# Two gate tiles of a hybrid decoder layer stored without their sigmoid, which is applied when they are loaded

## The chip, the core and the metric

The kernel runs on one core of a Trainium2 chip. Its engines are TensorE (PE, matrix products; PEld is its weight load), VectorE (DVE), ScalarE (ACT, elementwise functions by tables), GpSimd (POOL) and SyncE (SP, which here issues most transfers). Each engine takes its own instructions in order and waits on semaphores for the others. The metric is the device time of one execution in microseconds; lower is better.

## The reference

One decoder layer over 1024 positions of width 1024, in float32: a half feed-forward, two token mixers side by side, another half feed-forward, and a gated input embedding. The change lies in the gates that join the two mixers:

```python
fq, fk, fv, f_logit, sq, sk, sv, g_fox, g_sb = split_columns(h @ w_in[i])
...
y_fox = forgetting_attention(fq, fk, fv, log_f)      # 8 heads, softmax with forget gates
y_sb = stick_breaking_attention(sq, sk, sv)          # 8 heads, sigmoids and a running product
merged = (jax.nn.sigmoid(g_fox) * (y_fox @ w_branch_fox[i])
          + jax.nn.sigmoid(g_sb) * (y_sb @ w_branch_sb[i]))
x = x + merged @ w_out[i]
```

`g_fox` and `g_sb` have 1024 columns each. The forgetting heads (called fox heads in the kernel) need exponentials for their softmax; the stick-breaking heads need sigmoids; both gates need sigmoids.

## The kernel before

Everything is float32 split into a high and a low part, so that a product is three products of parts; the split is a cast on ScalarE and a subtraction on VectorE or GpSimd. The stages are: first feed-forward, mixer inputs, attention, merging of the branches, output projection, second feed-forward, embedding.

*Gates.* The 2048 gate columns are 16 tiles of 128 columns by 1024 positions, numbered 0 to 7 for `g_fox` and 8 to 15 for `g_sb`. Tiles 0 to 11 are made ahead of attention. Tiles 12 to 15 are made inside attention, as filler: `g_units(m)` makes tile `m` in two halves of 512 positions. For each half, 24 products (L807) gather in a PSUM bank, ScalarE turns the bank into a tile PT by a sigmoid (L926), and SP stores PT to the DRAM buffer `gates` (L927). The next user of that PSUM bank waits for L926.

*Attention.* Sixteen heads follow each other, heads 0 to 7 forgetting, 8 to 15 stick-breaking. In a fox head, scores (L1050, L1051) are added and their extremes taken on VectorE (L1055), ScalarE takes the exponential of a row block (L1061), VectorE the reciprocal of its sum (L1062), GpSimd multiplies (L1063). The weights are transposed on TensorE (L1109) into one of two PSUM banks of tag `pt`, ScalarE casts the bank to the high part (L1111), VectorE subtracts to get the low part (L1117) and so frees the bank, and TensorE multiplies with the values (L1135). Sums of two parts of an output are joined by L1161 and L1164. The stacks of queries and keys of later heads are filled by transposes (L897), L884, L885 and small copies on SP's queue (L887).

To keep TensorE fed between the dependent steps of a head, each head has a list `fill` of other units of work, of which some products are issued at each step. Tile 12 stands in the list of head 3, tile 13 in those of heads 6 and 7, tiles 14 and 15 in those of stick-breaking heads.

*Order.* The feed-forwards and the first gates are in an order written out by hand. In attention and the merging stage a planner orders the instructions of each engine by priorities and its own costs; for TensorE the program's order is pinned (`pe`), and for ScalarE and VectorE parts of the stick-breaking heads, the gate function among them (`order("act", ...)`). Tiles come from pools with tags and a fixed number of buffers (PT has 4, T 6, KL and Q 2); a tile waits for the last reader of the buffer that it gets.

*Tables.* ScalarE computes a function from a loaded table. Where the next function is not in the table in place, the build puts a load (ACT_TABLE_LOAD) ahead of it. A copy or cast needs none.

*Merging.* After attention, `load_gate(m)` loads tile 8+m into a buffer of tag T, or KL for m = 4 and Q for m = 5 (L1495). For each m the products of the stick-breaking branch (L1397) gather in a bank, VectorE multiplies the loaded gate with it (L1515) and adds the forgetting branch (L1516). The forgetting branch itself has its gates loaded by L1402 and multiplied by L1403.

Of the kernel before, what the change touches and what calls it, by code (L numbers as in the profile page):

```python
# [13 lines left out]
AF = mybir.ActivationFunctionType  # L14
# [8 lines left out]
KD = D // P  # L23
# [13 lines left out]
def tile_hybrid_decoder_layer(  # L37
# [6 lines left out]
    nc = tc.nc  # L44
# [11 lines left out]
    def slot(tag, shape, dt=F32):  # L56
        pad = -shape[-1] % 16
        t = sb.tile([*shape[:-1], shape[-1] + pad], dt, tag=tag, bufs=BUFS[tag], name=nm(tag))
        return t[:, :, :shape[-1]] if pad else t

    def stat(shape, tag, bufs=4):
        return st.tile(shape, F32, tag=tag, bufs=bufs, name=nm(tag))
# [3 lines left out]
    def bank(tag):  # L66
        return pp.tile([P, 512], F32, tag=tag, bufs=PSUM[tag], name=nm("ps"))

    def ps1():
        ring[0] += 1  # L70
        return bank(("pt", "pf", "pt", "pf")[ring[0] % 4])
# [11 lines left out]
    def order(key, ins):  # L83
        prev = last.get(key)
        if prev is not None and not manual[0]:
            tc.add_manual_dep(ins.ins, prev.ins.name, NOSYNC, reason="order")
        last[key] = ins
# [23 lines left out]
    def wload(pieces, nk, n, tags=("WH", "WL"), eng_lo=nc.gpsimd):  # L111
        return wsplit(wraw_load(pieces, nk, n), nk, n, tags, eng_lo)
# [31 lines left out]
    def kp(w):  # L144
        return w.rearrange("(k p) n -> p k n", p=P)
# [645 lines left out]
    def mix_nat(cols, tags):  # L791
        n = sum(b - a for a, b in cols)
        return [wload([kp(win)[:, 4 * kh:4 * kh + 4, a:b] for a, b in cols], 4, n, tags[kh]) for kh in range(2)]

    def nat_steps(ps, t, w, n, hT):
        i = 0
        for a, b in ((0, 0), (1, 0), (0, 1)):
            for k in range(KD):
                pe(nc.tensor.matmul(ps[:, :n], hT[t // 4](a, k)[:, (t % 4) * P:(t % 4 + 1) * P], w[k // 4][b][:, k % 4, :n], start=(i == 0), stop=(i == 23)))  # L799
                i += 1  # L800
                yield 0.109

    def feat_steps(ps, half, w):
        i = 0
        for a, b in ((0, 0), (0, 1), (1, 0)):
            for k in range(KD):
                pe(nc.tensor.matmul(ps[:], w[a][:, k, :], hT[half](b, k), start=(i == 0), stop=(i == 23)))  # L807
                i += 1
                yield 0.216
# [3 lines left out]
    def add_load(cell, fn):  # L813
        cell["i"] = len(loads)
        loads.append([cell, fn])

    def weights(cell, ahead=2):
        for i in range(cell["i"] + ahead):
            if i < len(loads) and loads[i][1] is not None:
                loads[i][0]["w"] = loads[i][1]()  # L820
                loads[i][1] = None
        return cell["w"]
# [9 lines left out]
    def v_units(col, extra, cell, new_bank=fill_bank):  # L832
        n = 256 + extra
        add_load(cell, lambda: mix_nat([(col, col + n)], NAT))

        def unit(t):
            weights(cell)
            if t == 0:
                cell["v"] = slot("X", [P, NT, 4, P], F32R)
            ps = new_bank()  # L840
            yield from nat_steps(ps, t, cell["w"], n, hT)
            v2 = cell["v"]
            src = ps[:, :256].rearrange("p (h d) -> p h d", h=4)
            split(v2[:, t, :, 0:HD], v2[:, t, :, HD:P], src, nc.scalar, nc.vector)
            if extra:
                nc.vector.tensor_copy(lfs[:, t, :], ps[:, 256:264])
        return [(24 * 0.109, unit(t)) for t in range(NT)]

    def fox_qk_units(pair, cell, tags=NAT, sq_tag="PT", new_bank=fill_bank):
        add_load(cell, lambda: mix_nat([(FQ + pair * P, FQ + pair * P + P), (FK + pair * P, FK + pair * P + P)], tags))  # L850

        def unit(t):
            weights(cell)
            if t == 0:
                cell["n"] = [slot("RN", [P, 4, 2, 2, HD]) for _ in range(2)]
                cell["ss"] = [stat([P, 4, 4], "qkss", 4) for _ in range(2)]
            half, q = divmod(t, 4)
            ps = new_bank()
            yield from nat_steps(ps, t, cell["w"], 256, hT)
            N = cell["n"][half]  # L860
            src = ps[:, :256].rearrange("p (s h d) -> p s h d", s=2, h=2)
            sq = slot(sq_tag, [P, 256])
            nc.scalar.activation(sq[:].rearrange("p (h s d) -> p s h d", s=2, h=2), src, AF.Square)
            nc.scalar.copy(N[:, q].rearrange("p h s d -> p s h d"), src)  # L864
            nc.vector.reduce_sum(cell["ss"][half][:, q, :], sq[:].rearrange("p (g d) -> p g d", g=4), axis=AX.X)
            if q == 3:
                ss = cell["ss"][half][:].rearrange("p a b -> p (a b)")
                nc.vector.tensor_scalar(ss, ss, 1.0 / HD, EPS, ALU.mult, ALU.add)
                nc.gpsimd.tensor_tensor(ss, ss, mhalf[:], ALU.pow)
                nv = N[:].rearrange("p a h s d -> p (a h s) d")  # L870
                nc.gpsimd.tensor_mul(nv, nv, ss.unsqueeze(2).broadcast_to([P, 16, HD]))
        return [(24 * 0.109, unit(t)) for t in range(NT)]
# [30 lines left out]
    def sb_stack_units(head, out_cell):  # L903
        c0 = head * HD

        add_load(out_cell, lambda: wload([kp(win)[:, :, SQ + c0:SQ + c0 + HD], kp(win)[:, :, SK + c0:SK + c0 + HD]], KD, P))

        def unit(half):
            weights(out_cell)
            if half == 0:  # L910
                out_cell["st"] = new_stacks()
            ps = bank("pf")
            yield from feat_steps(ps, half, out_cell["w"])
            fill_stacks(out_cell["st"], ps, slice(half * 512, half * 512 + 512))
        return [(24 * 0.216, unit(0)), (24 * 0.216, unit(1))]

    def g_units(m, new_bank=fill_bank):
        cell = {}

        add_load(cell, lambda: wload([kp(win)[:, :, GFOX + m * P:GFOX + m * P + P]], KD, P))  # L920

        def unit(half):
            ps = new_bank()
            yield from feat_steps(ps, half, weights(cell))
            g = slot("PT", [P, 512])
            order("act", nc.scalar.activation(g[:], ps[:], AF.Sigmoid))  # L926
            nc.sync.dma_start(gd[m, :, half * 512:half * 512 + 512], g[:])  # L927
        return [(24 * 0.216, unit(0)), (24 * 0.216, unit(1))]

# [330 lines left out]
    def attention():  # L1260
        fox_pairs = FOX_PAIRS
        vf1, vf0, vs0, vs1 = mx["v"], {}, {}, {}
        qk = [mx["qk"]] + [{} for _ in range(3)]
# [5 lines left out]
        def sst(h):  # L1269
            return sb_stack_units(h - 8, stacks[h])  # L1270
# [25 lines left out]
        f0 = fst(0, any_bank)  # L1296
        run_all(f0[:1] + p0[1:7] + f0[1:] + p0[7:] + p1)
        qk1, vx = fox_qk_units(fox_pairs[1], qk[1]), v_units(FV, 0, vf0)
        uq2, g12 = fox_qk_units(fox_pairs[2], qk[2]), g_units(12)
        uq3, vy = fox_qk_units(fox_pairs[3], qk[3]), v_units(SV, 0, vs0)  # L1300
        g13, s8, s9 = g_units(13), sst(8), sst(9)
        vz, s10, s11 = v_units(SV + 256, 0, vs1), sst(10), sst(11)
        s12, g14, s13 = sst(12), g_units(14), sst(13)
        s14, g15, s15 = sst(14), g_units(15), sst(15)
        fox_branch = fox_branch_units()
# [170 lines left out]
    nc.vector.tensor_scalar(gqk[0:HD, :], gqk[0:HD, :], HD ** -0.5, None, ALU.mult)  # L1476

    attention()

    od = dp.tile([4, P, 7, 512], F32, name="branch_sums")  # L1480
    xm = dp.tile([S, D], F32, name="x_mix")
    for m in range(5, KD):
        w = wload([kp(w_branch_fox[0])[:, :, m * P:(m + 1) * P]], 4, P)
        A.append(slot(("RN", "Q", "KH")[m - 5], [P, S]))
        for half in range(2):
            ps = bank(("sc", "sc", "sc", "pf", "pt", "pf")[2 * (m - 5) + half])
# [4 lines left out]
    gs = {}  # L1491

    def load_gate(m):
        gs[m] = slot(("T", "T", "T", "T", "KL", "Q", "T", "T")[m], [P, 2, 512])
        nc.sync.dma_start(gs[m][:], gd[KD + m].rearrange("p (h n) -> p h n", h=2))  # L1495
    load_gate(0)
    w = wload([kp(w_branch_sb[0])[:, :, 0:P]], 4, P)
    for m in range(KD):
# [12 lines left out]
        g = gs[m]  # L1511
        for half in range(2):
            ps = ps1()
# [161 lines left out]
```

## Time and profile before

| | |
|---|---|
| median of 3 runs | 2271.67 us (2269.41 to 2272.08) |
| profiled execution | 2270.58 us, of which the span of its instructions is 2268.9 us |
| granted TensorE clock, mean | 0.999 |
| TensorE busy | 2238.0 us, 99% |
| VectorE busy | 1484.3 us, 65% |
| ScalarE busy | 997.9 us, 44% |
| GpSimd busy | 801.7 us, 35% |
| gate sigmoids L926 | 8 of 598 ns, from 976.8 to 1332.8 us |

A profile's row in the groups reads: line, engine, operation, output tile <- input tile, shapes, count | busy time, mean duration in ns | idle time of the engine just before, and what ended it. A row of the timeline reads: start, duration, engine, line, operation, and in brackets the idle time before it with its releaser. Ends of matmuls are modelled. A wait for several semaphores is put down to the one that came last.

### The profile page before, as it was taken

What the parts mean: (1) busy time and instruction counts of PE and PEld (TensorE: products, weight loads), DVE (VectorE), ACT (ScalarE), POOL (GpSimd) and SP (SyncE); (2) the same over time, 40 slices, a digit from 0 to 9 for tenths busy, and PEclk for the clock granted to TensorE, in tenths of its full rate; (3) what the DMA queues carried; (4) which work ended last, traced back from release to release, by engine and by line L of the source; (5) the groups of instructions that cost most, each with busy time, mean ns of one, the idle gap of its engine ahead of it and who ended that gap; (6) DMA issues with size and microseconds to landing.
All of it is one profiled execution on the core that took longest, in us unless ns stands there. A gap on an engine that the chain in (4) does not pass through costs nothing.

```text
span 2268.9 us, 30821 instructions
## 1 busy us (share of the span) xinstructions
PE 2238.0 (99%) x11402; PEld 1902.5 (84%) x11402; DVE 1484.3 (65%) x2303; ACT 997.9 (44%) x1794; POOL 801.7 (35%) x803
## 2 busy tenths in 40 slices
PE   8999999999999999999999999999999999999999
PEld 6888888888888899989798888888888888888888
DVE  8845555688887325666578785789655555778753
ACT  6333333333364435565666663246333333434431
POOL 2444444300011236565566664410544444200121
PEclk9999999999999999999999999999999999999999
DMA  4232323484233333333324366822423232756132
GB/s 140 102 116 88 121 84 125 151 303 172 84 131 125 118 116 99 85 112 85 77 62 95 103 205 220 281 109 64 139 84 125 84 126 83 262 194 220 58 102 84
DMA packets 188936, 291.23 MB, mean 128 GB/s; under 512 B 28393, under 2 KB 104553, under 8 KB 188786
## 3 DMA queue, kind: packets, MB, share of 16 engines
q1 hardware_dynamic: 188784, 289.26, 38.5%
q8 instruction: 90, 1.47, 0.3%
q14 instruction: 60, 0.49, 0.1%
q10 hardware_dynamic: 2, 0.00, 0.0%
HBM read 193.50 MB, written 78.94 MB: 120 GB/s over the span
## 4 chain that ended last, share of the span: by engine, by line
PE 92%; DVE 4%; ACT 2%; issue 1%; DMA 0%; POOL 0%; SPq 0%; ACTq 0%; DVEq 0%; POOLq 0%
PE ps L556 39%; PE ps L454 21%; PE ps L799 7%; PE ps L807 5%; PE ps L1592 4%; PE ps L1397 4%; PE ps L1135 3%; PE ps L506 2%; PE ps L1109 2%; PE ps L1051 1%; PE ps L1050 1%; PE ps L956 1%; PE ps L228 1%; DVE PT L1117 1%; DVE RN L1013 1%
## 5 line engine op out<-in xcount | busy, mean ns | idle before, releaser
L454 PE MATMUL ps<-H,H 128*128 128x512 f32 x2184 | 497.7, 389 | 1.2 <-DVE X L462 1.2
L454 PEld LDWEIGHTS ps<-H,H 128*128 128x128 f32 x2184 | 409.4, 188 | 86.6 <-issue 2.0
L556 PE MATMUL ps<-H,WL 128*128 128x512 f32 x1116 | 264.9, 389 | 0.8 <-ACT WL L105 0.8
L556 PEld LDWEIGHTS ps<-H,WL 128*128 128x128 f32 x1116 | 209.4, 188 | 44.6 <-ACT WL L105 1.2
L556 PE MATMUL ps<-H,Q 128*128 128x512 f32 x612 | 146.0, 389 | 0.0
L462 DVE SCALAR_TENSOR_TENSOR X<-ps,X 128x512 f32<-128x512 f32 x168 | 109.0, 684 | 50.9 <-PE ps L454 50.9
L556 PEld LDWEIGHTS ps<-H,Q 128*128 128x128 f32 x612 | 114.9, 188 | 23.8
L556 PE MATMUL ps<-X,WL 128*128 128x512 f32 x552 | 132.6, 389 | 0.0
L139 POOL TENSOR_TENSOR WL<-RAW,WH 128x512 fp32r<-128x512 f32 (+1 forms) x84 | 98.6, 1196 | 68.0 <-ACT WH L129 42.5
L556 PEld LDWEIGHTS ps<-X,WL 128*128 128x128 f32 x552 | 103.6, 188 | 21.5
L1117 DVE TENSOR_TENSOR PT<-ps,PT 128x512 fp32r<-128x512 f32 (+1 forms) x160 | 100.1, 628 | 31.1 <-ACT PT L1111 30.2
L799 PE MATMUL ps<-WH,H 128*128 128x256 f32 x768 | 116.2, 288 | 1.0 <-ACT RN L864 0.8
L807 PE MATMUL ps<-H,WH 128*128 128x512 f32 x384 | 115.9, 409 | 0.0
L219 POOL TENSOR_SCALAR ss<-ss 128x1 f32<-128x1 f32 x28 | 9.0, 322 | 295.4 <-ACT WL L215 231.9
L1135 PE MATMUL ps<-PT,X 128*128 128x256 f32 (+1 forms) x640 | 102.8, 287 | 8.2 <-DVE PT L1117 5.5
L556 PE MATMUL ps<-H,PT 128*128 128x512 f32 x456 | 108.8, 389 | 0.0
L1111 ACT CAST PT<-ps 128x512 fp32r<-128x512 f32 (+1 forms) x160 | 87.2, 549 | 47.9 <-PE ps L1109 43.9
L1135 PEld LDWEIGHTS ps<-PT,X 128*128 128x128 f32 x640 | 90.7, 191 | 18.6 <-DVE PT L1117 10.2
L799 PEld LDWEIGHTS ps<-WH,H 128*128 128x128 f32 x768 | 101.4, 190 | 3.1 <-ACT RN L864 1.2
L556 PEld LDWEIGHTS ps<-H,PT 128*128 128x128 f32 x456 | 85.5, 188 | 17.7
L1063 POOL TENSOR_TENSOR T<-T,l 128x128 f32<-128x128 f32 (+3 forms) x64 | 73.3, 1149 | 76.0 <-DVE l L1062 75.8
L355 POOL TENSOR_TENSOR PT<-GF,RN 128x512 f32<-128x512 f32 x20 | 33.7, 1687 | 185.4 <-DVE GF L710 185.4
(435 smaller groups left out, 4896.6 us busy)
## 6 DMA issues: line engine op xcount, KB each, us to landing
hidden<-PT SPq DMA_DIRECT2D x40, 512.0 KB, 3.1
WH<-in_ffn_w_gate_dram SPq DMA_DIRECT2D x38, 512.0 KB, 5.5
Q<-hidden SPq DMA_DIRECT2D x24, 512.0 KB, 5.4
hidden<-RN SPq DMA_DIRECT2D x22, 512.0 KB, 2.6
KH<-in_ffn_w_up_dram SPq DMA_DIRECT2D x20, 512.0 KB, 6.3
KL<-in_ffn_w_up_dram SPq DMA_DIRECT2D x20, 512.0 KB, 6.9
T<-in_ffn_w_down_dram SPq DMA_DIRECT2D x20, 512.0 KB, 7.4
X<-in_x_dram SPq DMA_DIRECT2D x16, 512.0 KB, 10.2
```

Of the source, the lines that this page charges most:

```text
L139: ins = eng_lo.tensor_sub(lo[part], raw[part], f(hi[part]))
L454: pe(nc.tensor.matmul(groups[g][t][:], act[:, a, k, t * P:(t + 1) * P], wt[:, b, k, :], start=(fresh and n == 0), stop=(i in (6, 1, 4) and ...
L462: nc.vector.scalar_tensor_tensor(xs, groups[g][t][:], scale, xs, ALU.mult, ALU.add)
L556: pe(nc.tensor.matmul(ps[:], hl[:, a, k, :], rhs(m, b, k), start=(first and i == 0), stop=(final and i == 11), skip_group_check=True))
L799: pe(nc.tensor.matmul(ps[:, :n], hT[t // 4](a, k)[:, (t % 4) * P:(t % 4 + 1) * P], w[k // 4][b][:, k % 4, :n], start=(i == 0), stop=(i == ...
L807: pe(nc.tensor.matmul(ps[:], w[a][:, k, :], hT[half](b, k), start=(i == 0), stop=(i == 23)))
L1063: nc.gpsimd.tensor_mul(T[:, :n], T[:, :n], l[:].broadcast_to([P, n]))
L1111: high = nc.scalar.copy(pt[:, 0, :width], ps[:, :width])
L1117: ins = nc.vector.tensor_sub(pt[:, 1, :width], ps[:, :width], f(pt[:, 0, :width]))
L1135: pe(nc.tensor.matmul(o, lh, r, start=(kpair == c and i == 0), stop=(kpair == 0 and i == 3)))
L1397: pe(nc.tensor.matmul(ps[:], w[a][:, k, :], yT[g][b][:, k, half * 512:half * 512 + 512], start=(i == 0), stop=(i == 11)))
L1592: pe(nc.tensor.matmul(ps, hT[t // 4](a, k)[:, (t % 4) * P:(t % 4 + 1) * P], pl["w"][d, k // 2][b][:, k % 2, cs], start=(i == 0), stop=(i = ...
```

## The change

For tiles 12 and 13 the function that makes the gate copies the PSUM bank to PT in place of taking the sigmoid, and stores that. When such a tile is loaded for merging, ScalarE takes the sigmoid in place over the whole tile, 128x1024. Tiles 14 and 15 are as before.

```diff
+    raw_gates = []
+
-    def g_units(m, new_bank=fill_bank):
+    def g_units(m, new_bank=fill_bank, raw=False):
         cell = {}
+        if raw:
+            raw_gates.append(m)
...
             g = slot("PT", [P, 512])
-            order("act", nc.scalar.activation(g[:], ps[:], AF.Sigmoid))
+            order("act", nc.scalar.copy(g[:], ps[:]) if raw else nc.scalar.activation(g[:], ps[:], AF.Sigmoid))
             nc.sync.dma_start(gd[m, :, half * 512:half * 512 + 512], g[:])
...
-        uq2, g12 = fox_qk_units(fox_pairs[2], qk[2]), g_units(12)
+        uq2, g12 = fox_qk_units(fox_pairs[2], qk[2]), g_units(12, raw=True)
...
-        g13, s8, s9 = g_units(13), sst(8), sst(9)
+        g13, s8, s9 = g_units(13, raw=True), sst(8), sst(9)
...
     def load_gate(m):
         gs[m] = slot(("T", "T", "T", "T", "KL", "Q", "T", "T")[m], [P, 2, 512])
         nc.sync.dma_start(gs[m][:], gd[KD + m].rearrange("p (h n) -> p h n", h=2))
+        if KD + m in raw_gates:
+            nc.scalar.activation(gs[m][:], gs[m][:], AF.Sigmoid)
```

## The prediction

> **What bounds the kernel now.** The page comes first: TensorE is busy for 99% of the span and the chain that ended last is 92% TensorE. Time is therefore won only where TensorE stands idle.
>
> ```profile
> span 2268.9 us, 30821 instructions
> ...
> PE 92%; DVE 4%; ACT 2%; issue 1%; DMA 0%; POOL 0%; SPq 0%; ACTq 0%; DVEq 0%; POOLq 0%
> ```
>
> The view of waits, for TensorE alone, shows where: among its longest entries are attention's transposes (L1109) and value products (L1135), behind ScalarE's casts (L1111) or VectorE's reciprocals (L1062).
>
> ```profile
> PE ps L1109 <- DVE l L1062: 2.9, 2, 2.0
> PE ps L1135 <- ACT PT L1111: 2.1, 3, 1.6
> ```
>
> The groups of ScalarE give the prices. Eight table loads stand at the sigmoids and exponentials the change touches (four before L926, four before the next L1061); each is 1283 ns. The copy of the same shape (L962) is as long as a sigmoid, and an in-place pass over 128x1024 (L701) is 1061 ns.
>
> ```profile
> L701 ACT ACTIVATE GF<-GF 128x1024 f32<-128x1024 f32 x20 | 21.2, 1061 | 87.3 <-DVE GF L694 87.3
> ...
> L962 ACT COPY PT<-ps 128x512 f32<-128x512 f32 x16 | 9.4, 587 | 10.2 <-PE ps L956 9.9 <-ACT PT L962 0.3
> ...
> L884 ACT ACTIVATE KH<-ps,gqk 128x512 fp32r<-128x512 f32 x16 | 11.1, 693 | 0.7 <-PE ps L897 0.6
> ...
> L926 ACT ACT_TABLE_LOAD x4 | 5.1, 1283 | 1.6 <-issue 1.5
> L1061 ACT ACT_TABLE_LOAD x4 | 5.1, 1283 | 0.1
> ...
> L926 ACT ACTIVATE PT<-ps 128x512 f32<-128x512 f32 x8 | 4.8, 598 | 3.2 <-PE ps L807 3.2
> ```
>
> **The change part by part.** The order of the built program has, on ScalarE, the eight loads gone, four sigmoids turned into copies, and two 128x1024 sigmoids added without a table load (sigmoid is then the table in place). TensorE's order is unchanged. ScalarE loses 8 x 1.283 = 10.3 us, the copies save 4 x 0.011 us, and 2 x 1.06 us come back later. What this is worth must be read at each of the four places.
>
> *Tile 13, second half.* The timeline at 1097 us, ScalarE and TensorE:
>
> ```profile
> 1097.97 1.28 ACT L926 ACT_TABLE_LOAD   x1
> ...
> 1099.27 0.60 ACT L926 ACTIVATE PT<-ps 128x512 f32<-128x512 f32 x1
> ...
> 1099.34 0.60 PE L1109 MATMUL ps<-identf,T 128*128 128x128 f32 x4
> ...
> 1099.88 1.28 ACT L1061 ACT_TABLE_LOAD   x1
> ...
> 1101.18 0.72 ACT L1061 ACTIVATE T<-T,m 128x512 f32<-128x512 f32 x1
> ...
> 1101.90 1.05 ACT L1111 CAST PT<-ps 128x512 fp32r<-128x512 f32 x2
> ...
> 1102.49 1.29 DVE L1117 TENSOR_TENSOR PT<-ps,PT 128x512 fp32r<-128x512 f32 x2 [0.31 <-ACT PT L1111]
> ...
> 1102.51 0.39 PE L1135 MATMUL ps<-PT,X 128*128 128x256 f32 x1 [1.64 <-ACT PT L1111]
> ...
> 1103.24 0.62 PE L1135 MATMUL ps<-PT,X 128*128 128x256 f32 x3 [0.34 <-DVE PT L1117]
> ```
>
> The value product at 1102.51 waits for the first of the casts (1101.90), which stands behind load, sigmoid, load and exponential. Without the loads the gate copy runs 1097.97 to 1098.56, the first cast follows as soon as its transposes allow (about 1098.9), VectorE's low half is done by 1100.5, and TensorE, which arrives at 1100.9, waits for neither: 1.64 + 0.34 = 2.0 us. The exponential then runs between the two casts (new order), the second cast ending near 1101.0, before its product. Next late is nothing within 1 us.
>
> This idle time seems to have a second price. The view by windows, all engines (TensorE's busy time is the second figure, the granted clock the third from the end):
>
> ```profile
> 1100.45:1103.86 3.41, 1.43 (x9) 1.03 (x8) 1.45 (x3) 2.49 (x5) 2.08 (x4) 1.00 0.66 161
> 1103.86:1107.28 3.42, 3.42 (x14) 3.05 (x13) 0.39 (x1) 0.37 (x1) 0.00 (x0) 0.50 0.34 75
> 989.68:993.09 3.41, 1.37 (x12) 1.20 (x11) 2.81 (x8) 2.99 (x8) 1.09 (x3) 1.00 0.48 94
> ```
>
> Right after the window with 1.43 us of work, TensorE runs 3.42 us at half the clock, packed with work: 3.42 x 0.5 = 1.7 us lost. With the wait gone I expect the half clock gone too: 1.7 us. The third row, as idle and at full clock afterwards, says that idleness alone does not decide. The Trainium skill, "TensorE: Matmul & The Clock Gate", section "Part 1: The HAM clock gate", explains this by a free-running window of 3413 ns; the trace agrees in the length of the slow stretch.
>
> *Tile 12, second half.* ScalarE and TensorE at 985 us:
>
> ```profile
> 985.46 1.28 ACT L926 ACT_TABLE_LOAD   x1
> ...
> 987.40 0.66 PE L897 MATMUL ps<-identf,RN 128*128 128x128 f32 x4 [0.50 <-ACT PT L926]
> ...
> 988.34 1.28 ACT L1061 ACT_TABLE_LOAD   x1
> ...
> 988.86 0.71 PE L799 MATMUL ps<-WH,H 128*128 128x256 f32 x4 [0.23 <-DVE KL L885]
> ...
> 992.05 0.55 DVE L1117 TENSOR_TENSOR PT<-ps,PT 128x384 fp32r<-128x384 f32 x1
> ...
> 992.75 0.63 PE L1109 MATMUL ps<-identf,T 128*128 128x128 f32 x4 [2.04 <-DVE l L1062]
> ```
>
> ```profile
> 985.46:991.72 6.26, 4.35 (x33) 3.63 (x31) 3.90 (x12) 6.17 (x11) 4.97 (x5) 1.00 0.09 13
> 987.96:992.61 4.65, 2.52 (x20) 2.14 (x18) 3.90 (x11) 4.59 (x10) 2.47 (x3) 1.00 0.25 42
> ```
>
> ScalarE works 6.17 of 6.26 us here, 2.57 of them in loads; TensorE idles 0.50 + 0.23 + 2.04 = 2.8 us. The last wait is in truth for VectorE's L1117 at 992.05, which frees the PSUM bank of the transposes. Without the loads ScalarE stops being the packed one and VectorE takes over: before and with L1117 it must do the work of the second row, 3.90 us, and can begin when ScalarE's L884 (693 ns in the groups) ends, at 985.46 + 0.60 + 0.69 = 986.75. With some 0.3 us of gaps L1117 ends near 990.95 and TensorE restarts there instead of at 992.75: 1.8 us. Bounds: 1.28 (only one load's worth) to 2.8 (all idle).
>
> *Tile 13, first half.*
>
> ```profile
> 1088.25 1.28 ACT L1061 ACT_TABLE_LOAD   x1
> ...
> 1090.07 0.48 ACT L1111 CAST PT<-ps 128x384 fp32r<-128x384 f32 x1
> ...
> 1091.29 0.63 PE L1109 MATMUL ps<-identf,T 128*128 128x128 f32 x4 [0.91 <-DVE l L1062]
> ```
>
> Two loads stand ahead of the cast at 1090.07; it moves up 2.4 us, VectorE reads the bank before TensorE wants it: 0.9 us, all of the idle. *Tile 12, first half:* no TensorE wait near it is over 0.3 us; I count nothing.
>
> *Queues and other engines.*
>
> ```profile
> 990.06 0.39 SPq L119 DMA_DIRECT2D RAW<-in_w_in_dram  x1
> ...
> 1028.07 2.00 ACT L129 CAST WH<-RAW 128x1024 fp32r<-128x1024 f32 x2 [1.15 <-PE ps L799]
> ```
>
> On SP's queue the second store of each tile, and for tile 12 the stack copies behind it, no longer stand behind a weight load (for tile 12 the one at 990.06, which moves ten places back). The first casts of loaded weights after it are at 1028.07 and wait for TensorE, not for a load: 0. Were that cover gone, the load would be late by the ten issues ahead of it, which is still inside 38 us. The reordered reciprocals, bank reads (VectorE) and one mask addition (POOL) are among the work counted above.
>
> *The two added sigmoids.* Tile 12's goes through KL, tile 13's through Q. Each waits for its load, and ScalarE takes nothing else meanwhile. In the new order KL's stands right before the cast at 1384.73:
>
> ```profile
> 1384.73 0.59 ACT L1111 CAST PT<-ps 128x512 fp32r<-128x512 f32 x1 [1.18 <-PE ps L1109]
> ...
> 1388.20 1.11 PE L1135 MATMUL ps<-PT,X 128*128 128x256 f32 x8
> ```
>
> ```profile
> DMA  8898999999999597969679897777333111000447
> ...
> Q<-gates SPq DMA_DIRECT2D x1, 512.0 KB, 4.3
> ...
> L1515 DVE TENSOR_TENSOR Q<-Q,ps x2: 686/688/689, 1437.5 to 1440.2; 128x512 f32<-128x512 f32 x2
> ```
>
> The first line, the DMA share in 40 slices of 1378.9 to 1387, still moves data until the slices of zeros near 1385.8, so I take KL's landing as 1385.2 to 1386.3. Sigmoid to 1387.4 at the latest, cast 0.59, low half 0.69: 1388.7. The product that reads it is the second half of the eight at 1388.20, from 1388.65. Cost 0 to 0.1 us, and beyond that one for one with any further lateness; for the range I let it be 2. Q's load, in a window from 1416, lands 4.3 us after its issue, and VectorE multiplies that tile only at 1437.5 (third line, by source line): nothing.
>
> **Sum**, against the profiled execution's 2270.58 us: 2.0 + 1.7 + 1.8 + 0.9 = 6.4, less 0.1, gives 2264.3. The median of the runs shown, 2271.67, is 1.1 above that execution; I put the forecast at 2264.5.
>
> A rule to weigh: the Trainium skill, "ScalarE: Activation LUTs", section "What ACT_TABLE_LOAD costs", adds a drain of about 1380 ns to each load, 2.66 us in all. By that ScalarE would lose 21 us, and the sum would take the whole idle time of the three places, 2263.2 as an estimate. The trace disagrees: the sigmoid at 1099.27 starts 0.02 us after its load ends.
>
> **The rivals.**
> *The half clock is a matter of phase.* The rows above show a window as idle as the throttled one (1.37) at full clock, so the slow stretch may be absent in most timed runs of before, or fall elsewhere after. Then the gain is 4.6: 2266.0. That section of the Trainium skill on the clock gate speaks for it: its window runs free of the kernel.
> *The waits are handed on.* VectorE was 3.90 of 4.65 us busy at tile 12 and SP's copies shift; if a VectorE or bank wait takes back half of 4.7 and no clock gain comes: 2268.2. Against it, in the second half of tile 13 VectorE has 1.45 of 3.41.
> *KL's load lands late.* ScalarE stands, the casts and value products behind it, and TensorE loses each us past 1386.3. To end slower than before by the bound below, it must land 11 us later still, at 1397; the queues are all but still by 1385.8, so only another order of loads does it: about 2276.
> *The change does nothing*, if all loads were hidden: 2270.6; the waits quoted at L926 and L1111 speak against it.
>
> **How the numbers follow.** Forecast 0.63, phase 0.17, handed on 0.11, late 0.06, nothing 0.03. A measurement here tells 0.2%, about 4.5 us, from no change; against 2271.67 faster begins at 2267.1. Faster: 0.63, most of phase (0.12). Same: the rest of phase, handed on, nothing (0.19). Slower: 0.06. The range runs from every idle microsecond won (2.0 + 1.7 + 2.8 + 0.9, and 0.7 of small waits nearby: 2262.5) to handed on with the median's 1.1 (2269.3).
>
> **What would show it.** Right: eight table loads fewer and none at L926; TensorE's waits on L926 gone, that on L1111 under 1 us; no granted clock of 0.50 near 1100 us; fox heads about 6 us shorter; ScalarE idle before the new sigmoid for 1.5 to 3 us by the DMA, and the L1135 behind it without a wait above 0.3. Wrong: TensorE idle moved to L1135 near 1380, a half-clock stretch elsewhere, or VectorE waits at 990 that keep 992.75's row in place.

## The result and the profile after

The changed kernel takes 2263.77 us (median), the kernel before, run beside it, 2270.18 us: a ratio of 0.9969, 95% interval 0.9958 to 0.9980 (the two medians alone would give 0.9972). That is some 0.3% faster; the interval lies wholly below 1 and ends just at the 0.2% that the prediction took as the least that can be told. The forecast was 2264.5. The profiled execution of after took 2264.10 us. One of the eight executions of after took 5905.21 us, for a reason that nothing on record shows, and is left out of the ratio.

The page of after, first line and the line of busy times. TensorE's busy time fell by 2.3 us (2238.0 before) and the span by 6.5: the rest was time without TensorE work.

```profile
span 2262.4 us, 30810 instructions
...
PE 2235.7 (99%) x11402; PEld 1900.8 (84%) x11402; DVE 1486.8 (66%) x2303; ACT 989.3 (44%) x1788; POOL 801.2 (35%) x803
```

The groups of ScalarE of after. L926 is now L930, L1061 is L1065, L1111 is L1115, L1135 is L1139, and the new sigmoid is L1501. The eight table loads at the gate's line and at the exponential behind it are gone (the loads left stand at other lines). The last figures of the L1501 rows say that both new sigmoids waited for their DMA.

```profile
L930 ACT ACTIVATE PT<-ps 128x512 f32<-128x512 f32 x4 | 2.4, 598 | 3.2 <-PE ps L807 3.2
L930 ACT COPY PT<-ps 128x512 f32<-128x512 f32 x4 | 2.4, 589 | 2.0 <-issue 1.5 <-PE ps L807 0.4
...
L1501 ACT ACTIVATE Q<-Q 128x1024 f32<-128x1024 f32 x1 | 1.1, 1067 | 2.8 <-DMA Q<-gates 2.8
L1501 ACT ACTIVATE KL<-KL 128x1024 f32<-128x1024 f32 x1 | 1.1, 1062 | 3.7 <-DMA KL<-gates 3.7
```

TensorE's waits in after (us in total, times, longest). No wait on the gate's line is left, none on the reciprocal (2.9 us before), and the one on the casts went from 2.1 to 0.6. One wait grew: transposes on VectorE's subtraction, 4.3 us.

```profile
PE ps L1139 <- DVE PT L1121: 5.8, 13, 1.3
PE ps L1113 <- DVE PT L1121: 4.3, 6, 1.2
...
PE ps L1139 <- ACT PT L1115: 0.6, 2, 0.5
```

TensorE issues the same 11402 matmuls in the same order in every kernel of this study, so each can be set against the same matmul of the profile of before. The table gives by how much the distance changes across a place (us, minus is time won). The places are named by the times of before; each cell is the difference of two matmuls' starts, so the half clock stands in its own column.

| profile of | tile 12, second half (985 to 992.8) | 992.8 to 999.8 | tile 13, first half (1090 to 1095) | tile 13, second half (1100.6 to 1103.2) | half clock (1103.2 to 1108.4) | KL's sigmoid (1385 to 1394.9) |
|---|---|---|---|---|---|---|
| predicted | -1.8 | 0 | -0.9 | -2.0 | -1.7 | 0 to +0.1 |
| after | -2.00 | 0.00 | -0.88 | -2.40 | -1.66 | +0.81 |
| after, again | -1.99 | 0.00 | -0.88 | -2.40 | -1.66 | 0.00 |
| late | -2.01 | -0.01 | -0.88 | -2.40 | -1.66 | 0.00 |
| late, again | -2.00 | -0.01 | -0.88 | -2.40 | -1.67 | +0.02 |
| none | -2.00 | 0.00 | -0.89 | -2.40 | -1.66 | +0.01 |
| only 12 | -2.01 | 0.00 | +0.02 | 0.00 | -0.01 | +0.01 |
| only 13 | 0.00 | **+1.50** | -0.90 | -2.40 | -1.66 | +0.01 |
| half of 13 | -0.01 | 0.00 | +0.01 | -2.41 | -1.67 | +0.01 |
| exponential | -2.00 | 0.00 | -0.88 | -2.40 | -1.66 | 0.00 |
| dummy loads | -0.05 | **+1.52** | -0.99 | +0.04 | -1.58 | **+3.93** |
| all four | -2.01 | -0.01 | -0.88 | -2.40 | -1.66 | +0.11 |

What is not in the table is a distance of up to 0.8 us at 985, most of it from the start, and a few steps of 0.1 to 0.5 us at places that the change does not touch. One small step does belong to the change: at tile 12's first half (977.4) every profile without that tile's loads wins 0.18 us, and gives back 0.15 at 1052.4. Four columns carry the gain: 2.00 + 0.88 + 2.40 + 1.66 = 6.9 us, of which 0.8 go again at KL's sigmoid in this one profile.

*Tile 13, second half.* The timeline of after (start, duration):

```profile
1094.68 0.60 ACT L930 COPY PT<-ps 128x512 f32<-128x512 f32 x1
...
1095.73 0.58 ACT L1115 CAST PT<-ps 128x512 fp32r<-128x512 f32 x1 [0.45 <-PE ps L1113]
...
1096.40 0.69 DVE L1121 TENSOR_TENSOR PT<-ps,PT 128x512 fp32r<-128x512 f32 x1
1096.52 0.72 ACT L1065 ACTIVATE T<-T,m 128x512 f32<-128x512 f32 x1 [0.21 <-DVE m L1059]
1097.08 1.12 PE L1139 MATMUL ps<-PT,X 128*128 128x256 f32 x8
...
1097.24 0.57 ACT L1115 CAST PT<-ps 128x512 fp32r<-128x512 f32 x1
```

The copy stands 3.29 us earlier than the load did (1097.97). With 3.29 added, the first cast starts at 1099.02 (predicted about 1098.9), VectorE's low half ends at 1100.38 (1100.5), the exponential lies between the casts, and the second cast ends at 1101.10 (1101.0). The value products run as eight without a break. Two things differ from before here: the loads are gone, and the first cast stands ahead of the exponential, where before it stood behind it.

*Tile 12, second half.* The timeline of after, ScalarE, VectorE and TensorE: VectorE has become what TensorE waits for, as predicted.

```profile
985.54 0.69 ACT L884 ACTIVATE KH<-ps,gqk 128x512 fp32r<-128x512 f32 x1
...
986.27 0.75 DVE L885 SCALAR_TENSOR_TENSOR KL<-ps,gqk,KH 128x512 fp32r<-128x512 f32 x1 [0.62 <-ACT KH L884]
...
988.58 1.08 DVE L1175 TENSOR_TENSOR Y<-Y,PT 128x512 fp32r<-128x512 f32 x1
989.59 0.15 DVE L1066 RECIPROCAL l<-l 128x1 f32<-128x1 f32 x1
989.67 0.53 DVE L1121 TENSOR_TENSOR PT<-ps,PT 128x384 fp32r<-128x384 f32 x1
...
990.34 0.63 PE L1113 MATMUL ps<-identf,T 128*128 128x128 f32 x4 [1.19 <-DVE PT L1121]
```

VectorE begins behind L884 and works through to the subtraction that frees the bank, 986.27 to 990.20 = 3.93 us (predicted: 3.90 of work and 0.3 of gaps). Of TensorE's 2.8 us of idle time at this place 1.19 are left behind VectorE: this is the wait that grew in the view of waits. The planner's order of VectorE, ScalarE and SP is another here than before, as it is in every kernel without tile 12's loads.

*Tile 13, first half.* The cast that stood at 1090.07 is at 1085.88 in the timeline of after, which is 2.28 us ahead at this point: it moved up by 1.9 us (predicted 2.4). VectorE follows it, and no matmul between 1085 and 1090 waits:

```profile
1085.88 0.48 ACT L1115 CAST PT<-ps 128x384 fp32r<-128x384 f32 x1
...
1086.39 0.56 DVE L1121 TENSOR_TENSOR PT<-ps,PT 128x384 fp32r<-128x384 f32 x1 [0.34 <-ACT PT L1115]
```

*The clock.* Windows of after as long as those shown of before (TensorE's busy time is the second figure, the granted clock the third from the end): the place that ran at 0.50 before, and the place of tile 12, which has 2.21 us of TensorE work where it had 1.37.

```profile
1094.60:1098.00 3.40, 3.40 (x26) 3.14 (x25) 2.44 (x8) 2.55 (x6) 3.40 (x5) 1.00 0.20 77
1098.00:1101.40 3.40, 3.40 (x22) 3.00 (x21) 1.86 (x7) 0.37 (x1) 1.45 (x3) 1.00 0.80 159
988.80:992.20 3.40, 2.21 (x19) 2.03 (x19) 2.96 (x8) 1.78 (x5) 1.91 (x5) 1.00 0.90 272
```

*The two new sigmoids.* The timelines of after: ScalarE's rows around KL's sigmoid, the one TensorE row that waits, SP's issue of KL's load, and Q's sigmoid.

```profile
1375.67 0.59 ACT L1115 CAST PT<-ps 128x512 fp32r<-128x512 f32 x1
1379.91 1.06 ACT L1501 ACTIVATE KL<-KL 128x1024 f32<-128x1024 f32 x1 [3.66 <-DMA KL<-gates]
1380.88 1.05 ACT L1115 CAST PT<-ps 128x512 fp32r<-128x512 f32 x2
...
1382.22 0.61 PE L1139 MATMUL ps<-PT,X 128*128 128x256 f32 x3 [0.34 <-DVE PT L1121]
...
1371.65 0.42 SPq L1499 DMA_DIRECT2D KL<-gates  x1
...
1415.28 1.07 ACT L1501 ACTIVATE Q<-Q 128x1024 f32<-128x1024 f32 x1 [2.81 <-DMA Q<-gates]
```

KL's sigmoid starts 8.26 us after the issue and holds up two casts; TensorE loses 0.8 us, more than the 0.1 allowed. The wait for Q is hidden: no TensorE row waits between 1415 and 1445. What remained to settle was whether the loads made the gain, whether the half clock is a cost of this place or of chance, and what KL's sigmoid costs.

### The profile page after: what moved, and what is told of

Its sections match the earlier page's. It is cut to its first block, busy times and chain, and to the rows that moved or that the text cites. A ratio compares the mean times of both kernels' runs of the same rounds, so it can differ in the third digit from the quotient of the medians.

```text
span 2262.4 us, 30810 instructions
## 1 busy us (share of the span) xinstructions
PE 2235.7 (99%) x11402; PEld 1900.8 (84%) x11402; DVE 1486.8 (66%) x2303; ACT 989.3 (44%) x1788; POOL 801.2 (35%) x803
## 5 line engine op out<-in xcount | busy, mean ns | idle before, releaser
L807 PE MATMUL ps<-H,WH 128*128 128x512 f32 x384 | 115.1, 406 | 0.0
L1139 PE MATMUL ps<-PT,X 128*128 128x256 f32 (+1 forms) x640 | 102.7, 286 | 6.9 <-DVE PT L1121 5.8
L1115 ACT CAST PT<-ps 128x512 fp32r<-128x512 f32 (+1 forms) x160 | 87.1, 548 | 42.2 <-PE ps L1113 40.7
L1139 PEld LDWEIGHTS ps<-PT,X 128*128 128x128 f32 x640 | 90.3, 190 | 17.6 <-DVE PT L1121 10.8
```

The costliest lines, as they stand in the source:

```text
L1115: high = nc.scalar.copy(pt[:, 0, :width], ps[:, :width])
L1139: pe(nc.tensor.matmul(o, lh, r, start=(kpair == c and i == 0), stop=(kpair == 0 and i == 3)))
```

## The experiments

The first four ran on one chip, with 22 executions of before between them (median 2270.17), the next four on another (23 of before, 2270.08), the last two on a third (12 of before, 2270.01).

### The sigmoid behind the casts (late)

```diff
         if KD + m in raw_gates:
-            nc.scalar.activation(gs[m][:], gs[m][:], AF.Sigmoid)
+            order("act", nc.scalar.activation(gs[m][:], gs[m][:], AF.Sigmoid))
```

> The changed kernel, with its two late sigmoids pinned behind the last cast of attention's transposes on ScalarE; no other instruction moves. If the 0.76 us that TensorE lost near 1382 us came from ScalarE standing before the load of KL with two casts queued behind it, this wait is gone, the steps of the alignment with the kernel before end near -7.0 us, and the time is about 2263.0 against 2270.2. If the loss came from elsewhere (contention of transfers, GpSimd), the step of +0.7 stays and the time is that of the changed kernel, 2263.8.

Measured: 2263.15 us (2262.86 to 2263.27), ratio 0.9969 (0.9957 to 0.9981). In the built program the sigmoid of KL stands behind the two last casts, as ScalarE's timeline of late shows:

```profile
1379.26 0.59 ACT L1115 CAST PT<-ps 128x512 fp32r<-128x512 f32 x1 [1.70 <-PE ps L1113]
1379.74 1.06 ACT L1501 ACTIVATE KL<-KL 128x1024 f32<-128x1024 f32 x1
```

It finds its data there, and the step of 0.8 us is gone from the profile. That the time is 0.6 below that of the changed kernel proves nothing yet: that one comes from another set of executions (the last pair below).

### No sigmoid at all (none)

```diff
-        if KD + m in raw_gates:
-            nc.scalar.activation(gs[m][:], gs[m][:], AF.Sigmoid)
```

The sigmoid of tiles 12 and 13 is left out of the computation.

> The changed kernel without the two late sigmoids: tiles 12 and 13 stay without their sigmoid, so that part of the computation is left out. It prices the added work: 0.76 us at the load of KL and nothing at Q, so about 2263.0 and no step near 1382 us. If the added work costs more than the alignment shows (later stages), the time is below 2262.5.

Measured: 2263.06 us (2262.82 to 2263.30), ratio 0.9968 (0.9956 to 0.9981). Late, with both sigmoids, is 0.09 us longer, less than the spread of either: once they stand behind the casts, two passes of 1.06 us on ScalarE are free as far as can be told.

### One tile alone (only 12, only 13)

```diff
-        g13, s8, s9 = g_units(13, raw=True), sst(8), sst(9)
+        g13, s8, s9 = g_units(13), sst(8), sst(9)
```

> Only tile 12 is stored without its sigmoid. By the table loads: steps of -0.8, -0.4 and -0.9 us near 990 us, +0.8 near 1382, none at 1091 and 1102; sum -1.4 us, so about 2268.8. The wait of 1.64 us at 1102 stays, and the stretch of half clock after it comes or not with the phase. If the gain were the planner's new order or the stores' place on SP's queue rather than the loads, the steps near 990 would be smaller than 2.2 us in sum.

```diff
-        uq2, g12 = fox_qk_units(fox_pairs[2], qk[2]), g_units(12, raw=True)
+        uq2, g12 = fox_qk_units(fox_pairs[2], qk[2]), g_units(12)
```

> Only tile 13 is stored without its sigmoid. By the table loads: steps of -0.9 near 1091 us and -2.4 near 1102 us, and -1.5 where before was at half clock in its profile; none at 990 and none at 1382, since tile 13 is loaded to Q. Sum -3.3 to -4.8 us, about 2265.5 to 2267. If the half clock follows from the wait at 1102 it is absent here too; if it is phase alone, it can show at 990, where the wait of 2 us stays.

Measured: tile 12 alone 2267.89 us (2266.72 to 2269.23), ratio 0.9989 (0.9980 to 0.9998); tile 13 alone 2265.86 us (2264.84 to 2266.89), ratio 0.9980 (0.9971 to 0.9989). In the table each keeps its own places and gives up the other's: the places do not help each other. Two things were not as expected. With tile 12 alone KL's sigmoid costs nothing in its profile. And the half clock does not stay where it was. With tile 13 alone it is gone at 1103, but another has come right behind tile 12's wait (the view by windows of only 13, same columns as above):

```profile
990.20:993.70 3.50, 1.48 (x13) 1.30 (x13) 2.73 (x6) 2.41 (x6) 1.36 (x3) 1.00 0.65 140
993.71:997.12 3.41, 3.41 (x18) 3.41 (x17) 0.69 (x1) 0.59 (x1) 0.52 (x2) 0.50 0.90 332
```

TensorE's work there is what it was in the profile of before, where the clock stayed at 1.00. With tile 12 alone, the stretch stands behind tile 13's wait, here at 1102.31 where before had it at 1103.86 (windows of only 12):

```profile
1098.90:1102.31 3.41, 1.65 (x8) 1.32 (x9) 1.45 (x3) 1.84 (x5) 1.44 (x2) 1.00 0.82 194
1102.31:1105.72 3.41, 3.41 (x13) 3.02 (x12) 1.43 (x7) 0.37 (x1) 0.00 (x0) 0.50 0.18 42
```

So each of the two waits can bring a half-clock stretch, and need not. The timed executions bear it out. Each lists its mean granted clock, to three digits; a stretch of 3.41 us at half speed takes 0.00075 off the mean:

| kernel | executions: mean clock, median us | | |
|---|---|---|---|
| before (57) | 13: 1.000, 2268.43 | 29: 0.999, 2270.08 | 15: 0.998, 2271.52 |
| only 12 (10) | 3: 1.000, 2266.74 | 7: 0.999, 2268.10 | |
| only 13 (10) | 5: 1.000 (one 0.999), 2265.09 | 5: 0.999, 2266.70 | |

Before has two such places and three groups of times, 1.65 and 1.44 us apart; with one place left there are two groups, 1.4 and 1.6 apart. A half clock at the very end of the span, where TensorE has no work left, lowers this mean too (in after, 0.50 in the last 2 us), so the groups are told apart by their times: the execution of only 13 at 2264.84 us has a mean of 0.999 and stands among those at 1.000. That the groups are executions with no, one and two stretches is read from these counts and from the profiles; a stretch was seen only where an execution was profiled.

### The loads put back (dummy loads)

Ahead of each raw copy, a sigmoid over one column forces the table to be changed and changed back; the copies and the late sigmoids stay.

```diff
             g = slot("PT", [P, 512])
+            if raw:
+                order("act", nc.scalar.activation(stat([P, 1], "tiny")[:], ps[:, 0:1], AF.Sigmoid))
             order("act", nc.scalar.copy(g[:], ps[:]) if raw else nc.scalar.activation(g[:], ps[:], AF.Sigmoid))
```

> The changed kernel with a sigmoid of one element per partition put ahead of each of the four copies, its result unused. It brings the eight table loads back; the copies, the raw store and the two late sigmoids stay, and SP, GpSimd and TensorE stand in the order of the kernel before. If the loads are the cause, the gain is gone: no step of more than 0.3 us at 990, 1091 and 1102, about 0.2 us more per place for the small sigmoid, and the late sigmoid's +0.8: 2270.5 to 2272. If the copies or what is stored made the gain, it stays near 2264.

Measured: 2269.71 us (2268.47 to 2273.11), ratio 0.9999 (0.9990 to 1.0009): the gain is gone. By the table it is gone at two of the three places. One place keeps 0.99 us, and in the profile KL's sigmoid loses more than that; that the same holds in the other executions is likely, but not shown. The groups of ScalarE show the loads back:

```profile
L931 ACT ACT_TABLE_LOAD x4 | 5.1, 1283 | 0.1
L1067 ACT ACT_TABLE_LOAD x4 | 5.1, 1283 | 0.1
```

Its profile (2273.11 us, its longest execution) misses the expectation in two places, as ScalarE's timeline, one TensorE row and, below them, a row of before show. At tile 13's first half the 0.99 us stay won: the load there starts right behind the exponential (second row), where the load of before stood idle for 1.46 us first ("[1.46 <-issue]" at 1085.95 in its timeline). The view of L926 in before shows what held it: a wait instruction of 2778 ns, the longest of seven (last row; this one stands from 1083.14 to 1085.92). ScalarE waits there, for the products of L807, before it reaches the load. The one-column sigmoid has no such wait instruction. Its load runs during the wait, and it waits itself, 0.14 us, behind the load. A load that fitted into a wait cost nothing here. And KL's sigmoid waits 5.35 us for a load that takes 9.98 us from its issue at 1377.62 on; TensorE stands 1.61 us for the cast behind it, and a half-clock stretch follows at 1389.68 (not shown). That is the 3.93 of the table, and the rival "KL's load lands late" as it was described.

```profile
1085.56 0.19 ACT L1067 ACTIVATION_READ_ACCUMULATOR T<-T,m 128x1 f32 x1
1085.77 1.28 ACT L931 ACT_TABLE_LOAD   x1
1087.19 0.17 ACT L931 ACTIVATE tiny<-ps 128x1 f32<-128x1 f32 x1
...
1387.60 1.06 ACT L1503 ACTIVATE KL<-KL 128x1024 f32<-128x1024 f32 x1 [5.35 <-DMA KL<-gates]
...
1389.18 0.38 PE L1141 MATMUL ps<-PT,X 128*128 128x256 f32 x1 [1.61 <-ACT PT L1117]
```

```profile
L926 ACTq EVENT_SEMAPHORE  x7: 17/17/2778, 985.4 to 1332.7; - x7
```

### The loads taken away in another way (exponential)

The kernel before, with an exponential in place of the sigmoid of tiles 12 and 13. It needs the table that is in place; there is no copy and no later sigmoid, so the gate's sigmoid is left out of the computation.

```diff
-    def g_units(m, new_bank=fill_bank):
+    def g_units(m, new_bank=fill_bank, fn=AF.Sigmoid):
...
-            order("act", nc.scalar.activation(g[:], ps[:], AF.Sigmoid))
+            order("act", nc.scalar.activation(g[:], ps[:], fn))
...
-        uq2, g12 = fox_qk_units(fox_pairs[2], qk[2]), g_units(12)
+        uq2, g12 = fox_qk_units(fox_pairs[2], qk[2]), g_units(12, fn=AF.Exp)
...
-        g13, s8, s9 = g_units(13), sst(8), sst(9)
+        g13, s8, s9 = g_units(13, fn=AF.Exp), sst(8), sst(9)
```

> The kernel before with an exponential in place of the sigmoid of tiles 12 and 13, and no sigmoid later (the gates of these tiles are left wrong, so their sigmoid is not computed). An exponential takes the same pass through ScalarE as the sigmoid and no table load, so this takes the loads away and changes nothing else but the planner's order. By the loads: about 2263.1, the time without the late sigmoids. If a copy were cheaper than a table function behind a PSUM bank, it is slower than that by more than 0.5 us.

Measured: 2263.18 us (2262.88 to 2263.27), ratio 0.9967 (0.9955 to 0.9979), with the steps of the changed kernel to the hundredth. So neither the copies nor the form of the stored gate matter. What this kernel shares with the changed one is the absence of the loads, and one thing more: wherever a place's loads go, the planner also orders VectorE, ScalarE or SP's queue near it in the new way, and this kernel has that order as well, while the one with the dummy loads has almost that of before. Order and loads come together in all these runs.

### Half a tile (half of 13)

```diff
-            order("act", nc.scalar.copy(g[:], ps[:]) if raw else nc.scalar.activation(g[:], ps[:], AF.Sigmoid))
+            order("act", nc.scalar.copy(g[:], ps[:]) if raw and half else nc.scalar.activation(g[:], ps[:], AF.Sigmoid))
...
-        uq2, g12 = fox_qk_units(fox_pairs[2], qk[2]), g_units(12, raw=True)
+        uq2, g12 = fox_qk_units(fox_pairs[2], qk[2]), g_units(12)
...
-            nc.scalar.activation(gs[m][:], gs[m][:], AF.Sigmoid)
+            nc.scalar.activation(gs[m][:, 1, :], gs[m][:, 1, :], AF.Sigmoid)
```

> Only the second half of tile 13 is stored without its sigmoid (taken later over that half). It removes the two loads around 1098 and 1100 us alone: a step of -2.4 us at 1102, none at 990 and 1091, time by full clock 2268.4 - 2.2 = about 2266.2. The half clock may still follow the wait at 992, not the one at 1102: runs fall in two groups 1.6 us apart, not in three.

Measured: 2266.26 us (2265.66 to 2267.70), ratio 0.9985 (0.9975 to 0.9994), six executions from 2265.66 to 2266.27 and four from 2267.58 to 2267.70, the two expected groups. Two loads at one place give the whole 2.41 us of that place and nothing anywhere else, and apart from the late sigmoid the order of the engines differs from before nowhere else. At the place itself it does: the first cast stands ahead of the exponential, as in the changed kernel (timeline of half of 13; before has 1101.90 behind 1101.18).

```profile
1098.39 0.59 ACT L1115 CAST PT<-ps 128x512 fp32r<-128x512 f32 x1 [0.47 <-PE ps L1113]
...
1099.17 0.73 ACT L1065 ACTIVATE T<-T,m 128x512 f32<-128x512 f32 x1 [0.19 <-DVE m L1059]
```

No run takes the loads away and keeps the old order, or the reverse, so what each is worth is an estimate. In the old order without loads the exponential could start near 1099.67, when the maxima that it needs are ready (row of before below), and the second group of value products came 2.06 us behind the exponential (1101.18 to 1103.24): at 1101.73, so 1.5 of the 2.4 us would be won. The other 0.9 would come of the cast passing the exponential. The new order with the loads left in would win something too, as the first products would no longer wait; but the second cast would stand behind the same work as in before, and end no earlier. At this place the gain is thus shown for loads and order together, not for the loads alone.

```profile
1099.57 0.08 DVE L1055 DVE_READ_ACCUMULATOR2_ANT m<- 128x1 f32 x1
```

### All four tiles (all four)

```diff
-            s12, g14, s13 = sst(12), g_units(14), sst(13)
-            s14, g15, s15 = sst(14), g_units(15), sst(15)
+            s12, g14, s13 = sst(12), g_units(14, raw=True), sst(13)
+            s14, g15, s15 = sst(14), g_units(15, raw=True), sst(15)
```

> All four tiles of attention stored without their sigmoid. Tiles 14 and 15 stand among sigmoids, so no table load goes; two more sigmoids over 128x1024 come at merging, in two T buffers. If the loads are the whole gain, this is no faster than the changed kernel: 2263.8, up to 0.5 slower where a T load comes late. If a copy in attention were worth something by itself, two times 0.9 us more.

Measured: 2263.34 us (2263.23 to 2263.71), ratio 0.9971 (0.9960 to 0.9983). Tiles 14 and 15 stand in heads that use the sigmoid's table anyway and had no loads to lose, so their raw store is worth nothing.

### The changed kernel and late on one chip (after again, late again)

> The changed kernel once more, beside the next one on the same chip. Both theories: 2263.2 to 2264.1, as in its seven undisturbed times so far. Theory A (the sigmoid of KL costs TensorE what its step showed): its profile has a step of about +0.76 us at the matmul that starts near 1382, with the sigmoid of KL waiting over 3 us for its DMA. Theory B (that wait is hidden in most executions): no such step here, as in the profile of only12.

> The sigmoid of KL issued behind the last two casts. Theory A: 0.4 to 0.8 us under the changed kernel on this chip, so 2262.8 to 2263.4, with no step near 1382. Theory B: within 0.3 us of the changed kernel.

Measured: 2263.16 us (2262.87 to 2264.32), ratio 0.9971 (0.9960 to 0.9982), and 2263.13 us (2262.65 to 2263.56), ratio 0.9970 (0.9959 to 0.9982). The two are equal. Theory A falls: in the new profile of the changed kernel KL's sigmoid waits again, but starts 7.02 us after its issue, not 8.26, and TensorE loses nothing.

The timeline of SP, then that of ScalarE, in this second profile of the changed kernel:

```profile
1371.19 0.42 SPq L1499 DMA_DIRECT2D KL<-gates  x1
```

```profile
1378.21 1.06 ACT L1501 ACTIVATE KL<-KL 128x1024 f32<-128x1024 f32 x1 [2.41 <-DMA KL<-gates]
1379.17 1.05 ACT L1115 CAST PT<-ps 128x512 fp32r<-128x512 f32 x2
```

Their rows in the table say the same: the steps differ by 0.02 us at most. The 0.6 us by which late seemed better lies between two sets of executions of the same changed kernel (medians 2263.77 and 2263.16). What made them differ is open: the kernel before took 2270.18 and 2270.01 beside them, so it is not simply the chip, and a load of KL that landed late more often in the first set would do it too. On one chip late is no faster; it only does without the exposure to that load.

## Why the prediction was right

It was right in sign, in size (0.7 us off) and in the terms; two sizes were off by up to a fifth, and one term varies more than was allowed.

- *Tile 13, second half, 2.0 us:* 2.40. The chain came out as written, each start within 0.2 us. The profile of before credited TensorE with waits of 1.64 and 0.34; the starts of the same matmuls moved by 2.4, so the place held 0.4 us of idle time that no wait row showed (ends of matmuls are modelled, and an idle time is counted from such an end). The chain needed the new order as well as the absence of the loads: by the estimate above about 0.9 us of the 2.4 come of the cast standing ahead of the exponential, an order that the prediction had seen in the built program.
- *Tile 12, second half, 1.8 us of bounds 1.28 to 2.8:* 2.00. That VectorE takes over was right, with 1.19 us left behind it. The mis-sized part: VectorE had no gaps of 0.3 us, so TensorE restarts at 990.34, which with the 0.41 that after was ahead of before at 985 is 990.75 in the time of before, and not 990.95. VectorE's order changed here together with the loads, and no run separates the two at this place.
- *Tile 13, first half, 0.9 us:* 0.88. Part of it came without the loads going: with dummy loads in, the place still gave 0.99, since the first load there ran during the wait that held it back in before.
- *Half clock, 1.7 us:* 1.66 in the profiles, and right in the mean, though not as a fixed cost of this place. By the groups of before, 57 executions hold 29 + 2 x 15 = 59 stretches, about one each, of 1.4 to 1.7 us; that the profile of before, on which the sum was built, held one, the average number, was luck; it stands at one of the two places that can bring it. The rival *phase* had its premise right (tile 12's row at full clock is luck, as the profile with tile 13 alone shows), its result wrong: no stretch was seen without such a wait ahead of it. Of the changed kernel, late, none, exponential and all four not one profile has a stretch before the end (the emptiest 3.41 us there hold 2.01 to 2.03 us of TensorE work), and the times that enter their comparisons lie between 2262.65 and 2264.39. At full clock throughout, before takes 2268.43 and after 2263.16: 5.3 us, which are the 2.00 + 0.88 + 2.40.
- *The rule on the table loads' drain:* by it the sum was 2263.2 as an estimate. The time came out near that, but not by that rule: the extra gain is in the places' own sizes, and no load of before or of the dummy kernel has a drain behind it (the next instruction starts 0.01 to 0.15 us after the load's end).
- *KL's sigmoid, 0 to 0.1 us, up to 2 for the range:* 0 between the medians of the last pair, 0.8 in one profile of the changed kernel, 2.4 in that of the dummy loads. What failed is the landing: its latest time, 1386.3, was taken from when the DMA slices of one profile fell to zero. Set back to the time of before (by the shift ahead of the place: 7.76, 7.30 and 1.27 us), the sigmoid starts at 1385.97 in the second profile of the changed kernel, at 1387.21 in its first and at 1388.87 with the dummy loads. The costs are 0, 0.81 and, without the half clock, 1.78 + 0.61 = 2.39 us at the two matmuls that wait: within 0.2 us one for one with the lateness past 1386.3, as predicted. The rival *KL late* names a real mechanism, which shows where the load takes more than some 7.4 us from its issue (1378.95 to 1386.3).
- *Tile 12, first half:* 0.18 us won and 0.15 lost again later, as good as nothing.
- *The queues; Q; the copies:* nothing, as predicted.
- *The signs:* the loads, the waits on L926 and L1111 and the clock near 1100 came as named. In the first profile of after the new sigmoid waited 3.66 us instead of 1.5 to 3 and the product behind it 0.34 instead of 0.3 at most, which is the late load of KL; in the second it waited 2.41.
- *Handed on:* only the 1.19 us at tile 12, which the sum had.

## What to carry to other kernels

A table load costs what the engine that sets the pace waits at that place, not its 1.28 us: of eight loads (10.3 us of ScalarE) two at one place gave 2.4 us, two at another 0.9, two 2.0 and two 0.18, each together with the order that the planner made without them. Price each place by following its chain to the next engine's bound, and count a half-clock stretch as a cost of the wait ahead of it, weighted by how often it comes over many executions. A step that moves behind a load on an engine working in order should stand behind that engine's urgent work; and a difference of half a microsecond between kernels counts only if both were measured side by side: one kernel's medians over seven executions lay 0.6 apart.

## What the hardware showed that was not expected

- A wait of about 2 us can halve TensorE's clock for the 3.41 us that follow. The 3.41 us ahead of each of the five stretches seen hold 1.39 to 1.69 us of TensorE work (four profiles, before, only 12, only 13 and dummy loads). The Trainium skill, "TensorE: Matmul & The Clock Gate", section "HAM oscillation — how this bites in real kernels", gives as the rule no TensorE gaps over about 3.4 us. Here single gaps of 1.6 to 2.0 us were enough, so the measurement decides. In its section "Part 1: The HAM clock gate" the Trainium skill has the window run free of the kernel, and the three groups of times of before agree.
- The same load of 512 KB from DRAM, at the same place, took 7.0 to 10.0 us from issue to the sigmoid that waited for it in five profiles (7.0, 7.4, 7.6, 8.3 and 10.0), where the one for Q, issued in quieter surroundings, landed after 4.3 us in the profile of before.
- Executions of one kernel fall into groups 1.4 to 1.7 us apart, so a median over few of them moves by that much: the three first times of before, median 2271.67, lay 1.6 above the median of all later ones.
